# Seven-product jobs for the first half of layer 0's MLP, with the S5 tables built elsewhere

## The chip, the cores and the metric

The kernel runs on one core of one Trainium2 chip. The metric is the device time of one execution in microseconds (us). Before the change the median of 3 runs is 1545.18 us (1544.69 to 1546.54).

The core's engines work side by side, each through its own instruction list in order: PE (TensorE, matrix products into PSUM banks), DVE (VectorE), ACT (ScalarE), POOL (GpSimd) and SP (SyncE, which here only issues DMAs). An instruction that waits for another engine holds up all that stands behind it on its own engine.

## The reference

One inference step of a trunk with two layers over 544 columns (a prompt of 512 positions and 8 samples of 4), model width 1024. Layer 0 mixes tokens with a convolution module, layer 1 with a diagonal complex state-space layer (S5); each layer then has a cross-attention to a memory and an MLP with squared ReLU. All in fp32.

```python
def _s5(u, h0_re, h0_im, a_re, a_im, log_dt, b_re, b_im, c_re, c_im, d_skip, w_glu):
    dt = jnp.exp(log_dt.astype(f32))[:, None]
    mag = jnp.exp(dt * a_re)
    ab_re = mag * jnp.cos(dt * a_im)
    ab_im = mag * jnp.sin(dt * a_im)
    den = a_re * a_re + a_im * a_im
    num_re = ab_re - 1.0
    coef_re = (num_re * a_re + ab_im * a_im) / den
    coef_im = (ab_im * a_re - num_re * a_im) / den
...
def _sqrelu_mlp(xn, w_up, w_down):
    h = jax.nn.relu(jnp.einsum('bld,df->blf', xn, w_up))
    return jnp.einsum('blf,fd->bld', h * h, w_down)

def _trunk(x, conv_bufs, s5_re, s5_im, mem_k, mem_v, p):
    for i in range(DEPTH):
        h = _rmsnorm(x, p['norm_mix'][i])
...
        x = x + out
        x = x + _cross_attention(_rmsnorm(x, p['norm_xattn'][i]), mem_k[i], mem_v[i],
                                 p['xattn_w_q'][i], p['xattn_w_o'][i])
        x = x + _sqrelu_mlp(_rmsnorm(x, p['norm_ffn'][i]), p['mlp_w_up'][i], p['mlp_w_down'][i])
```

The powers of `ab` that S5's block form needs (its tables) depend on weights alone, and the kernel works them out while another stage runs.

## The kernel before

Activations lie transposed: the model width as 8 tiles of 128 partitions (`kt`, or `o` on the output side), the 544 columns along the free side. An fp32 product is made of three passes over pairs of a high and a low part (fp32r). A weight block of 128x1024 therefore gives 48 matmuls of 128x272 (8 k-tiles, 3 passes, 2 halves of the columns): this is called a gemm here.

**Weight blocks.** `run` (L140) goes through a written-out list of `Step`s. SP loads blocks of 512 KB into 6 buffers `wst` (L163), 4 blocks ahead of preparing. `prep_block` (L166) prepares a block up to two steps ahead: ACT copies the high part (L137), DVE subtracts for the low part (L177), into one of three `whl` tiles. After each step `pop_bg` lets background generators emit work up to a budget, `bg`, in their own units (about us of DVE).

**Attention.** q steps, then score steps, then the output product: `ofirst` (o = 0, 1) and `ofin(o)` (o = 2 to 7). Each `ofin` ends with `oend`: DVE adds the product to `x` (L1020), `norm_in` gives the MLP's input (ACT high part, DVE L253) and adds squares into `acc` (L262). The norm's statistic is a copy of `acc`'s last 32 columns on DVE (L284, `accs`) and a product with ones on PE (L287).

**MLP.** In layer 0 `mlp_layer` runs two halves, each 16 `up` gemms and 16 `dn` gemms. In layer 1 `seven_layer` does it with a seven-product scheme: a pair of up blocks takes 7 products of 12 matmuls (L1295) in place of 96 matmuls; the first pair stays plain (L1382); down gemms are at L1403. The sums of weights (L1176), low parts (L1168) and forms of the input (L1140 to L1143, L250) are DVE work. `us_early` prepares the first of them while the attention ends. All this is a list of jobs with an engine and a duration, put in order by a list scheduler (`planned`) whose order depends on the jobs' durations, not on the rest of the program.

**S5's tables.** `s5_prep` is a generator that runs as background in layer 0's MLP, at 3.2 a step from the first up step on. First come 143 small DVE operations on 128x32 (the scalars: dt, exponentials, sines, powers, `coef`, `unit`; L1590 to L1667). Then for each of 8 k-tiles: products on DVE (L1738 to L1763), 8 transposes on PE (L1780), 16 small matmuls (L1788), ACT copies, and rotations on DVE (L1813 to L1817, 7 levels of 4 operations, each level twice as wide). Three DMAs store E, Tst and C (L1801 to L1803), a fourth the rotations (L1819), to the DRAM tensor `tab`, which the S5 stage loads again.

## Time and profile before

| | |
|---|---|
| median of 3 runs | 1545.18 us |
| profiled execution | 1544.75 us |
| its span (first to last instruction) | 1543.0 us |
| PE busy | 1496.6 us, 97% |
| DVE busy | 1015.6 us, 66% |
| ACT busy | 685.0 us, 44% |
| POOL busy | 200.9 us, 13% |

The profiled execution is 1.75 us longer than its span. A busy share is a mean over the whole span; what an edit is worth is read in its own stretch. The stretches, in us from the start: layer 0's attention from 283 to 374.67 (from the scores on), then its output product and first MLP half to 615.17, the second half to 818.73, where the S5 stage begins; layer 1's output product and first two of four MLP quarters from 1113.82 to 1342.53. In timelines x48 is a number of instructions drawn together, and [1.82 <-ACT whl L137] the idle time ahead of them with what ended it.

### The profile page before, as it was taken

The page shows a single profiled execution, that of the slowest core. Times are in us where ns is not written, and L with a number is a line of the kernel's source. Part 1 is how long each engine was busy: PE and PEld are TensorE (multiplying, and loading weights), DVE is VectorE, ACT ScalarE, POOL GpSimd, SP SyncE. Part 2 cuts the span into 40 slices and gives each one's busy share as a digit, 9 for nine tenths or more (in the row PEclk, how much of TensorE's full clock was granted, in tenths as well). Part 3 has the DMA queues.
Part 4 walks back from the last instruction along what each step waited for, and adds up shares of the span by engine and source line. Part 5 has one row for each costly group of instructions (what it writes and reads, how often), then busy time and mean ns, then how long its engine had stood idle before and what let it go on. Part 6 is the DMA issues. An engine that isn't in the chain of part 4 may idle for free.

```text
span 1543.0 us, 29397 instructions
## 1 busy us (share of the span) xinstructions
PE 1496.6 (97%) x11949; PEld 1450.0 (94%) x11949; DVE 1015.6 (66%) x2094; ACT 685.0 (44%) x1274; POOL 200.9 (13%) x167
## 2 busy tenths in 40 slices
PE   8999979999999999999999999999999999999996
PEld 8999969898999999999998899998899999999996
DVE  6896786444576666666757964553479677685855
ACT  6332354343445433665443443343357445272642
POOL 2555550000000000000103750000000000000001
PEclk9999989999999999999999999999999999999998
DMA  8765526453223344433587974237322314141211
GB/s 278 191 156 136 185 82 219 150 220 133 101 83 103 134 134 134 134 134 116 170 271 226 340 237 182 110 138 271 125 69 85 135 55 151 42 146 47 92 46 59
DMA packets 92535, 224.49 MB, mean 145 GB/s; under 512 B 12496, under 2 KB 42976, under 8 KB 88304
## 3 DMA queue, kind: packets, MB, share of 16 engines
q1 hardware_dynamic: 87440, 211.06, 40.1%
q0 software_dynamic: 1792, 6.37, 2.3%
q10 hardware_dynamic: 3168, 5.18, 0.9%
q8 instruction: 94, 1.54, 0.4%
q14 instruction: 41, 0.34, 0.1%
HBM read 192.78 MB, written 29.80 MB: 144 GB/s over the span
## 4 chain that ended last, share of the span: by engine, by line
PE 78%; DVE 8%; ACT 1%; issue 1%; DMA 1%; POOL 0%; SPq 0%; DVEq 0%; POOLq 0%; ACTq 0%
PE banks L215 44%; PE banks L1403 12%; PE banks L1295 10%; PE banks L467 2%; PE banks L956 2%; PE banks L892 2%; PE banks L973 1%; PE banks L876 1%; PE banks L227 1%; PE banks L1382 1%; DVE banks L1958 1%; ACT slot L137 1%; DVE banks L702 1%; PE banks L1992 1%; PE banks L1780 0%
## 5 line engine op out<-in xcount | busy, mean ns | idle before, releaser
L215 PE MATMUL banks<-slot,whl 128*128 128x272 f32 x6264 | 805.0, 290 | 6.1 <-ACT slot L137 2.9
L215 PEld LDWEIGHTS banks<-slot,whl 128*128 128x128 f32 x6264 | 794.0, 189 | 11.4 <-ACT slot L137 4.8
L137 ACT ACTIVATE whl<-wst 128x1024 fp32r<-128x1024 f32 (+1 forms) x236 | 218.7, 930 | 132.8 <-PE banks L1403 47.8
L177 DVE TENSOR_TENSOR whl<-wst,whl 128x1024 fp32r<-128x1024 f32 x137 | 169.6, 1242 | 92.8 <-ACT whl L137 91.0
L1403 PE MATMUL banks<-slot,whl 128*128 128x272 f32 x912 | 120.2, 288 | 0.5 <-DVE rt L1316 0.5
L137 ACT ACTIVATE slot<-banks 128x512 fp32r<-128x512 f32 (+7 forms) x132 | 60.3, 480 | 135.5 <-PE banks L215 42.3
L1403 PEld LDWEIGHTS banks<-slot,whl 128*128 128x128 f32 x912 | 116.7, 188 | 0.7 <-DVE rt L1316 0.7
L1295 PE MATMUL banks<-slot,whl 128*128 128x272 f32 x756 | 97.2, 288 | 0.9 <-DVE tmp L1413 0.9
L1295 PEld LDWEIGHTS banks<-slot,whl 128*128 128x128 f32 x756 | 95.6, 188 | 1.1 <-ACT whl L137 1.1
L137 ACT ACTIVATE slot<-x,vec 128x544 fp32r<-128x544 f32 (+2 forms) x50 | 35.2, 727 | 108.7 <-DVE x L2027 43.8
L1413 DVE TENSOR_TENSOR tmp<-banks,rb 128x544 f32<-128x544 f32 x30 | 21.7, 724 | 83.0 <-PE banks L1403 83.0
L1403 PE MATMUL banks<-slot,arena_mlp 128*128 128x272 f32 x528 | 71.5, 288 | 0.4 <-DVE rt L1316 0.4
L1485 POOL MEMSET slot<- 128x128 f32 x1 | 0.2, 205 | 546.9 <-PE banks L1295 546.9
L702 DVE SCALAR_TENSOR_TENSOR banks<-slot,vec,banks 128x512 f32<-128x512 f32 x90 | 67.9, 755 | 2.8
L1403 PEld LDWEIGHTS banks<-slot,arena_mlp 128*128 128x128 f32 x528 | 68.2, 188 | 0.6 <-DVE rt L1316 0.6
L1295 PE MATMUL banks<-slot,arena_mlp 128*128 128x272 f32 x504 | 65.3, 288 | 0.4 <-DVE acc L1330 0.4
L1295 PEld LDWEIGHTS banks<-slot,arena_mlp 128*128 128x128 f32 x504 | 63.9, 188 | 0.7 <-DVE acc L1330 0.6
L137 ACT ACTIVATE tmp<-x 128x544 f32<-128x544 f32 x40 | 25.9, 648 | 65.0 <-DVE x L1099 39.7
L425 POOL TENSOR_TENSOR slot<-slot,slot 128x512 fp32r<-128x512 f32 x4 | 6.1, 1557 | 371.4 <-ACT slot L137 371.4
L137 ACT ACTIVATE tmp<-banks 128x544 f32<-128x544 f32 x32 | 19.9, 623 | 76.5 <-PE banks L215 76.5
L177 POOL TENSOR_TENSOR whl<-wst,whl 128x1024 fp32r<-128x1024 f32 x19 | 45.2, 2383 | 55.2 <-ACT whl L137 55.2
L250 DVE TENSOR_TENSOR slot<-tmp,slot 128x544 fp32r<-128x544 f32 x32 | 23.2, 726 | 41.5 <-ACT slot L137 41.5
(283 smaller groups left out, 2068.8 us busy)
## 6 DMA issues: line engine op xcount, KB each, us to landing
wst<-in_w SPq DMA_DIRECT2D x231, 512.0 KB, 4.4
arena_att<-in_kc SPq DMA_DIRECT2D x16, 1024.0 KB, 4.9
arena_att<-in_vc SPq DMA_DIRECT2D x16, 1024.0 KB, 5.3
tab<-arena_prep SPq DMA_DIRECT2D x24, 512.0 KB, 3.9
whl<-in_w POOLq DMA_DIRECT2D x12, 512.0 KB, 6.2
arena_s<-tab SPq DMA_DIRECT2D x8, 768.0 KB, 5.5
arena_s<-tab SPq DMA_DIRECT2D x8, 512.0 KB, 6.3
arena_s<-tab SPq DMA_DIRECT2D x12, 256.0 KB, 5.2
```

The lines of the kernel that those rows point to most:

```text
L137: self.nc.scalar.activation(out, in_, func, **kw)
L177: eng.tensor_sub(t[:, 1].bitcast(F32R), src, t[:, 0])
L215: self.nc.tensor.matmul(ps[:, c, :HALF], w, x[:, c * HALF : c * HALF + HALF], start=first and n == 0, stop=last and n == len(seq) - 1)
L227: self.nc.tensor.matmul(ps[:, c, :HALF], self.w8(b, kt)[wi], rhs[kt][xi].bitcast(F32R)[:, c * HALF : c * HALF + HALF], start=first and kt ...
L250: self.nc.vector.tensor_sub(l.bitcast(F32R), src_h if src_l is None else src_l, h)
L467: nc.tensor.matmul(ps[m], self.memt(2 * kp + k2, xi)[:, m * 128 : m * 128 + 128], t[:, wi, k2 * 512 : k2 * 512 + 512], start=kp == 0 and k ...
L702: nc.vector.scalar_tensor_tensor(A, win(k), w(k), A, op0=ALU.mult, op1=ALU.add)
L892: nc.tensor.matmul(o, qs[qi], ks[ki], start=e == 0 and i == 0, stop=e == 1 and i == 2)
L956: nc.tensor.matmul(ps[e], vs[vi], xs[xi], start=m == 0 and i == 0, stop=m == 1 and i == 2)
L1295: nc.tensor.matmul(bank, u[:, wi, k * 128 : k * 128 + 128], x[k][xi].bitcast(F32R), start=n == k == 0, stop=n == 2 and k == 3)
L1403: nc.tensor.matmul(ps[:, c, :HALF], us[kt // 4][:, wi, kt % 4 * 128 : kt % 4 * 128 + 128], M["h"][kt][xi].bitcast(F32R)[:, c * HALF : c * ...
L1413: job("V", 0.7, lambda: V.tensor_mul(self.c2(t), self.psv(ps), self.c2(self.rb)), [*bk, "rb"], [("t", o % 2)])
```

## The change

- Layer 0's first MLP half (up blocks 0 to 15, down blocks of the first half) becomes `seven_layer(0, 2)`, two quarters of the scheme of layer 1; the second half stays `mlp_layer`. The forms of the input and `us_early` now also run in layer 0's `ofin`. The up weights of that half are laid out on the host as layer 1's are.
- The scalars become a generator of their own, `s5_scalars`, background in layer 0's attention at 2.0 a step (q steps and `ofin` steps); a `pop_all` step empties it before the MLP. It uses two slots in place of the arena.
- The tables, `s5_prep`, run in the second half alone, at 5.8 a step.
- The rotations go to POOL: per k-tile 2 memsets and 28 operations, issued at the k-tile's start, and their DMA is issued there too, ahead of the k-tile's other three.

```diff
@@ oend, ofirst, ofin (layer 0 too) @@
-            if L and o % 2:
+            if o % 2:
                 self.seven_forms(o // 2)
...
-                if L and o > 5:
+                if o > 5:
                     self.us_early(2 * (o - 5))
@@ mlp_layer @@
-        for half in range(2):
-            self.steps += [up(16 * half + i) for i in range(16)]
-            self.steps += [dn(half, o, c) for o in range(8) for c in range(2)]
+        self.steps += [up(16 + i) for i in range(16)]
+        self.steps += [dn(1, o, c) for o in range(8) for c in range(2)]
@@ seven_layer @@
-    def seven_layer(self):
+    def seven_layer(self, L, quarters):
...
-        for q in range(4):
+        for q in range(quarters):
@@ s5_prep, at the start of each k-tile @@
+            W = nc.gpsimd
+            W.memset(rot[:, 0, :, 0:1], 1.0)
+            W.memset(rot[:, 1, :, 0:1], 0.0)
+            for lev in range(7):
+                n = 1 << lev
+                u = un[:, :, lev, qs].unsqueeze(3).to_broadcast([P, 2, 4, n])
+                m = rt[:, : 8 * n].rearrange("p (x q c) -> p x q c", x=2, q=4)
+                turn = lambda x: rot[:, x, :, 0:n].unsqueeze(1).to_broadcast([P, 2, 4, n])
+                new = rot[:, :, :, n : 2 * n]
+                W.tensor_mul(m, turn(1), u)
+                W.tensor_mul(new, turn(0), u)
+                W.tensor_sub(new[:, 0], new[:, 0], m[:, 1])
+                W.tensor_add(new[:, 1], new[:, 1], m[:, 0])
+            nc.sync.dma_start(tab[:, 2560:3584].rearrange("p (x q c) -> p x q c", x=2, q=4), rot)
@@ s5_prep, at the end of each k-tile @@
-            V.memset(rot[:, 0, :, 0:1], 1.0)
-            V.memset(rot[:, 1, :, 0:1], 0.0)
-            yield 0.2
-            for lev in range(7):
-                n = 1 << lev
...
-                V.tensor_mul(m[0], rot[:, :, :, 0:n], ub[0])
-                V.tensor_mul(m[1], rot[:, :, :, 0:n], ub[1])
-                yield 0.2 + 0.016 * n
-                V.tensor_sub(rot[:, 0, :, n : 2 * n], m[0][:, 0], m[1][:, 1])
-                V.tensor_add(rot[:, 1, :, n : 2 * n], m[0][:, 1], m[1][:, 0])
-                yield 0.2 + 0.008 * n
-            nc.sync.dma_start(tab[:, 2560:3584].rearrange("p (x q c) -> p x q c", x=2, q=4), rot)
@@ the program @@
-        begin, _, steps = self.att_layer(0, 0)
+        begin, _, steps = self.att_layer(0, 2.0)
         S.append(begin)
+
+        def background(work):
+            return Step(lambda: self.bgq.append(work()))
+        S.append(background(self.s5_scalars))
         S += steps
-
-        def start_prep():
-            self.bgq.append(self.s5_prep())
-        S.append(Step(start_prep))
-        self.mlp_layer(0, lambda k: self.sumsq(k, self.X[k]), 3.2)
+        S.append(Step(self.pop_all))
+        self.seven_layer(0, 2)
+        S.append(background(self.s5_prep))
+        self.mlp_layer(0, lambda k: self.sumsq(k, self.X[k]), 5.8)
```

The first place is DVE at the end of layer 0's attention. `x_74` is the last of the 8 `x` tiles, `accs` the copy for the norm's statistic. Before:

```order
L1020 TENSOR_TENSOR x_74<-x_74,banks 128x544
L253 SCALAR_TENSOR_TENSOR slot_4112<-x_74,vec,slot_4111 128x544
L262 TENSOR_TENSOR acc<-acc,tmp_87 128x544
L177 TENSOR_TENSOR whl_82<-wst_79,whl_82 128x1024
L284 COPY accs<-acc 128x4x4 x2
```

And now, from the two last rows of the work on the weights that stands behind `x_74`'s; `unit` and the two slots are the scalars':

```order
L1168 TENSOR_TENSOR arena_mlp_3821<-wst_78,arena_mlp_3821 128x512
L1168 TENSOR_TENSOR arena_mlp_3821<-wst_77,arena_mlp_3821 128x512
L1628 TENSOR_TENSOR slot_2716<-slot_2715 128x32
L1628 TENSOR_TENSOR slot_2715<-unit 128x32 x2
L1628 TENSOR_TENSOR unit<-slot_2715 128x32
L1689 COPY unit<-slot_2716 128x32
...
L1628 TENSOR_TENSOR slot_2716<-slot_2715 128x32
L1628 TENSOR_TENSOR slot_2715<-unit 128x32 x2
L1628 TENSOR_TENSOR unit<-slot_2715 128x32
L1689 COPY unit<-slot_2716 128x32
L284 COPY accs<-acc 128x4x4 x2
```

19 scalar operations now stand between the last row of `us_early` and L284, and 53 more behind the evacuations of o = 2 to 6 (10, 10, 11, 11, 11).

The second place is DVE at the last q step of layer 0's attention, where the attention norm's statistic is taken; `qz` holds copies of the query. Before:

```order
L177 TENSOR_TENSOR whl_82<-wst_76,whl_82 128x1024
L850 TENSOR_TENSOR slot_2766<-banks,slot_2765 128x544
L858 COPY qz_92<-banks 128x4x2 x4
L284 COPY accs<-acc 128x4x4 x2
L316 TENSOR_SCALAR sm_ms<-banks 128x5
```

Now:

```order
L856 TENSOR_TENSOR slot_2781<-banks,slot_2780 128x544
L864 COPY qz_92<-banks 128x4x2 x4
L1612 TENSOR_SCALAR slot_2715<-slot_2715 128x32 x2
L1614 TENSOR_SCALAR slot_2715<-slot_2715 128x32
L1648 CAST slot_2715<-slot_2715 128x32
L1612 TENSOR_SCALAR slot_2715<-slot_2715 128x32
L1628 TENSOR_TENSOR slot_2715<-slot_2715 128x32
L1628 TENSOR_TENSOR slot_2715<-slot_2715,slot_2716 128x32 x2
L1614 TENSOR_SCALAR slot_2715<-slot_2715 128x32
L1612 TENSOR_SCALAR slot_2715<-slot_2715 128x32
L1624 SCALAR_TENSOR_TENSOR slot_2715<-slot_2715 128x32
L284 COPY accs<-acc 128x4x4 x2
```

Here 11 scalar operations stand between the copies of the query and L284.

The third place is SP in the tables of one k-tile. Before, the rotations' DMA is L1819:

```order
L163 DMA wst_76<-in_w 128x1024
L163 DMA wst_77<-in_w 128x1024
L163 DMA wst_78<-in_w 128x1024
L163 DMA wst_79<-in_w 128x1024
L1801 DMA tab<-arena_prep 128x1024
L1802 DMA tab<-arena_prep 128x512
L1803 DMA tab<-arena_prep 128x8x128
L163 DMA wst_80<-in_w 128x1024
L163 DMA wst_75<-in_w 128x1024
L1819 DMA tab<-arena_prep 128x1024
```

Now it is L1779 and waits for POOL:

```order
L1757 DMA qz_91<-in_s5bc 128x256
L1779 DMA tab<-arena_prep 128x1024
L163 DMA wst_79<-in_w 128x1024
L163 DMA wst_80<-in_w 128x1024
L163 DMA wst_75<-in_w 128x1024
L1846 DMA tab<-arena_prep 128x1024
L1847 DMA tab<-arena_prep 128x512
L1848 DMA tab<-arena_prep 128x8x128
```

Three weight loads now stand behind each k-tile's rotations in SP's list.

## Rows read from the trace of the kernel before

**Rows 1.** The page: busy time, share and instructions of each engine; and the lines of the chain of work that ended last.

```profile
PE 1496.6 (97%) x11949; PEld 1450.0 (94%) x11949; DVE 1015.6 (66%) x2094; ACT 685.0 (44%) x1274; POOL 200.9 (13%) x167
PE 78%; DVE 8%; ACT 1%; issue 1%; DMA 1%; POOL 0%; SPq 0%; DVEq 0%; POOLq 0%; ACTq 0%
```

**Rows 2.** Windows: the stretch, its length, busy time (and instructions) of each engine, PE's granted clock, DMA share, GB/s. First layer 0's output product with its first MLP half, then its second half, then layer 1's output product with two quarters.

```profile
374.67:615.17 240.50, 240.50 (x1960) 239.11 (x1959) 156.54 (x456) 104.00 (x197) 0.00 (x0) 1.00 0.33 112
615.17:818.73 203.56, 201.67 (x1634) 200.07 (x1634) 127.29 (x320) 105.48 (x223) 6.32 (x6) 0.99 0.50 165
1113.82:1342.53 228.71, 224.14 (x1780) 223.03 (x1779) 165.76 (x298) 114.16 (x204) 0.00 (x0) 1.00 0.25 86
```

**Rows 3.** Timeline of DVE at the end of layer 1's attention: start, duration, what it is, idle time before it.

```profile
1131.12 0.71 DVE L1020 TENSOR_TENSOR x<-x,banks 128x544 f32<-128x544 f32 x1
...
1143.10 0.72 DVE L1020 TENSOR_TENSOR x<-x,banks 128x544 f32<-128x544 f32 x1 [0.28 <-PE banks L215]
1144.64 0.79 DVE L253 SCALAR_TENSOR_TENSOR slot<-x,vec,slot 128x544 fp32r<-128x544 f32 x1 [0.82 <-ACT slot L137]
...
1155.16 0.72 DVE L1020 TENSOR_TENSOR x<-x,banks 128x544 f32<-128x544 f32 x1 [1.86 <-PE banks L215]
...
1162.37 0.25 DVE L284 COPY accs<-acc 128x16 f32<-128x16 f32 x2
```

**Rows 4.** Timeline of PE at the same place.

```profile
1124.69 30.43 PE L215 MATMUL banks<-slot,whl 128*128 128x272 f32 x240 [1.82 <-ACT whl L137]
...
1162.93 0.36 PE L287 MATMUL banks<-ones,accs 128*128 128x2 f32 x2
```

**Rows 5.** Timeline of DVE in the scalars; nine other rows of lines L1606 and L1667 lie between the two, and the stretch from the start of the first to the start of the second has 14 operations.

```profile
466.50 0.18 DVE L1667 COPY unit<-arena_prep 128x32 f32<-128x32 f32 x1
...
468.91 0.17 DVE L1667 COPY unit<-arena_prep 128x32 f32<-128x32 f32 x1
```

**Rows 6.** Timeline of DVE and PE at layer 0's attention statistic.

```profile
284.46 0.24 DVE L284 COPY accs<-acc 128x16 f32<-128x16 f32 x2
...
283.77 1.05 PE L287 MATMUL banks<-ones,acc 128*128 128x2 f32 x8
284.76 0.38 PE L287 MATMUL banks<-ones,accs 128*128 128x2 f32 x2
```

**Rows 7.** Timeline of PE at the tables' transposes and small matmuls, of one k-tile in the first half and of one in the second; the last row is the second half's first gemms.

```profile
761.00 1.22 PE L1780 MATMUL banks<-ident,arena_prep 128*128 128x128 f32 x8 [1.89 <-ACT arena_prep L137]
...
607.51 1.03 PE L1780 MATMUL banks<-ident,arena_prep 128*128 128x128 f32 x8
608.30 6.28 PE L215 MATMUL banks<-slot,whl 128*128 128x272 f32 x48
614.51 0.67 PE L1788 MATMUL banks<-arena_prep 128*32 128x128 f32 x16
615.10 21.13 PE L215 MATMUL banks<-slot,whl 128*128 128x272 f32 x166
```

**Rows 8.** Windows of 2 us behind the idle time at 759 and behind that at 1122.87; the columns are those of rows 2.

```profile
761.00:763.00 2.00, 2.00 (x13) 2.00 (x14) 1.98 (x6) 1.98 (x6) 0.00 (x0) 0.71 1.03 296
763.00:765.00 2.00, 2.00 (x11) 2.00 (x11) 1.81 (x2) 1.38 (x2) 0.00 (x0) 0.50 0.93 340
765.00:767.00 2.00, 2.00 (x17) 2.00 (x17) 0.64 (x1) 0.00 (x0) 0.00 (x0) 0.94 0.07 27
...
1126.00:1128.00 2.00, 2.00 (x18) 2.00 (x17) 1.66 (x2) 0.30 (x1) 0.00 (x0) 1.00 0.52 184
```

**Rows 9.** Timeline of DVE in the tables: the low part of the first up product of the second half; the start of a k-tile's first table operation and of the work behind its 14th; the start of its 15th and of the work behind its 22nd.

```profile
623.48 0.73 DVE L250 TENSOR_TENSOR slot<-tmp,slot 128x544 fp32r<-128x544 f32 x1 [1.37 <-ACT slot L137]
...
595.82 0.22 DVE L1738 TENSOR_TENSOR arena_prep<-qz,arena_prep 128x64 f32<-128x64 f32 x1
...
598.99 1.23 DVE L177 TENSOR_TENSOR whl<-wst,whl 128x1024 fp32r<-128x1024 f32 x1
...
760.13 0.42 DVE L1752 TENSOR_TENSOR arena_prep<-qz,spw 128x256 f32<-128x256 f32 x1
...
763.02 1.23 DVE L177 TENSOR_TENSOR whl<-wst,whl 128x1024 fp32r<-128x1024 f32 x1
```

**Rows 10.** Groups of POOL's instructions: line, what it is, count, busy time and mean of one in ns; and one line's smallest, median and largest.

```profile
L632 POOL TENSOR_TENSOR slot<-slot,vec 128x496 f32<-128x496 f32 x10 | 11.7, 1187 | 2.9 <-DVE slot L538 2.9
...
L1971 POOL TENSOR_TENSOR sm<-slot,slot x16: 196/205/1190, 843.7 to 906.8; 128x4 f32<-128x4 f32 x16
```

**Rows 11.** Timeline of POOL and DVE at a place where both work: from the second row to the third DVE does four rotation operations of the widest level (two of 128x512, two of 128x256); then DVE alone with the same four.

```profile
745.46 6.11 POOL L425 TENSOR_TENSOR slot<-slot,slot 128x512 fp32r<-128x512 f32 x4 [371.39 <-ACT slot L137]
...
745.61 1.70 DVE L1813 TENSOR_TENSOR arena_prep<-arena_prep,unit 128x512 f32<-128x512 f32 x1
...
751.79 1.22 DVE L177 TENSOR_TENSOR whl<-wst,whl 128x1024 fp32r<-128x1024 f32 x1
...
787.34 0.69 DVE L1813 TENSOR_TENSOR arena_prep<-arena_prep,unit 128x512 f32<-128x512 f32 x1
...
789.35 1.22 DVE L177 TENSOR_TENSOR whl<-wst,whl 128x1024 fp32r<-128x1024 f32 x1
```

**Rows 12.** The page's DMA issues: count, KB each, median us from issue to landing.

```profile
wst<-in_w SPq DMA_DIRECT2D x231, 512.0 KB, 4.4
...
tab<-arena_prep SPq DMA_DIRECT2D x24, 512.0 KB, 3.9
```

More of the change, by code (lines that the diff above doesn't have):

```diff
@@ L102, in __init__ @@
         self.weave = deque()
+        self.seven = {}
         self.late = []
@@ L140, in run @@
     def run(self):
-        flat = self.flat = [b for s in self.steps for b in s.blocks]
-        npz, used = self.npz, 0
+        flat, used = self.flat, 0
         for s in self.steps:
-            used += len(s.blocks)
-            while npz < len(flat) and npz < used + self.NHL - 1 + s.deep and self.whl:
-                self.load_upto(npz + 1)
-                self.prep_block(flat[npz], npz)
-                npz += 1
-            self.load_upto(npz + self.ahead)
+            used += len(s.blocks) + len(s.raw)
+            while self.npz < self.limit and self.npz < used + self.NHL - 1 + s.deep and self.whl:
+                self.load_upto(self.npz + 1)
+                self.prep_block(flat[self.npz], self.npz)
+                self.npz += 1
+            self.load_upto(self.npz + self.ahead)
             s.fn()
@@ L160, in load_upto @@
     def load_upto(self, n, eng=None):
-        while self.nd < min(n, len(self.flat)):
+        while self.nd < min(n, self.limit):
             i = self.nd
@@ L359, in start @@
         nc, I = self.nc, self.I
-        self.flat = [b for s in self.steps for b in s.blocks]
+        self.flat, self.bases = [], []
+        for s in self.steps:
+            if s.raw:
+                self.bases.append(len(self.flat))
+            self.flat += s.blocks + s.raw
+        self.limit = self.bases[0]
         self.nd = 0
@@ L1250, in loads @@
         def loads():
-            while st["nub"] < len(self.ublocks) and ulast[st["nub"] - self.NST] < st["nu"]:
+            while st["nub"] < len(ublocks) + (0 if L else self.NST) and ulast[st["nub"] - self.NST] < st["nu"]:
                 g = st["nub"]
@@ L1257, in makes @@
             loads()
-            while st["nu"] < min(upto, len(self.uitems)):
+            while st["nu"] < min(upto, len(uitems)):
                 n = st["nu"]
-                kind, g, _ = self.uitems[n]
+                kind, g, _ = uitems[n]
                 w0, w1 = wkey(g), wkey(g + 1)
@@ L1414, in dn @@
             job("V", 0.7, lambda: V.tensor_add(self.X[o], self.X[o], t), [("t", o % 2)], [("x", o)])
-            if q == 3:
+            if L and q == 3:
                 t1 = ("t", 1 - o % 2)
@@ L1422, in seven_layer @@
         self.acc_e, self.acc_f = self.acc[:, lo], self.acc[:, hi]
-        for q in range(4):
+        for q in range(quarters):
             ps = list(range(4 * q, 4 * q + 4))
@@ L1721, in s5_prep @@
         rot = take(1, 1024).rearrange("p (x q c) -> p x q c", x=2, q=4)
+        rt = take(0, 512)
         nc.gpsimd.memset(gc, 0.0)
```

98 lines of the change are left out of this document (59 added, 39 removed).

## The prediction

> **What bounds the kernel now.** I read the page's busy times first, then the chain of waits, then windows of the stretches that change, then the timelines of PE and DVE at their edges. PE is busy for 97% of the span and makes up 78% of the chain [rows 1], so PE work saved is time saved, and an edit on another engine counts only where PE stands still for it. In the first MLP half of layer 0 PE doesn't stand still at all: 240.50 us busy of 240.50; in the second half it idles 1.89 us; in layer 1's equal stretch, which already runs the seven-product jobs, 4.57 of 228.71 [rows 2]. DVE looks free by share, 66%, but its work is bunched: at the end of layer 1's attention it waits for PE only twice between 1131 and 1162.37, for 0.28 and 1.86 us; its other pauses, 0.82 each, lie inside an evacuation, between L1020 and L253, where nothing that stands behind it can go [rows 3]. PE's product with `accs` starts 0.31 us after DVE's copy has ended (1162.62 and 1162.93), so DVE is just in time there [rows 3, 4]. The changed program puts 72 scalar operations into that very place of layer 0.
>
> **Attention.** 71 of the 143 scalars go into the q steps; where they fill DVE's pauses they cost nothing. Not so the 11 ahead of L284: the copy starts at 284.46 and PE's product with it at 284.76, while PE's products before it end at about 284.8 [rows 6], so the cover is about 0.1 us. A scalar takes 2.41 us / 14 = 0.172 us, start to start [rows 5]. That is 11 x 0.172 = 1.9, less 0.1: **+1.8**. After a stop of PE of this size the granted clock may fall: behind the 1.89 us at 759 three windows of 2 us show 0.71, 0.50 and 0.94, a loss of 2 x (0.29 + 0.50 + 0.06) = 1.7 us; behind the 1.82 us that end at 1124.69 the window shows 1.00 [rows 4, 7, 8]. 0.50 is the 1.2 GHz level, 1.00 the 2.4 GHz one. Two stops of one size with two answers: I take half, **+0.85**, bounds 0 and 1.7.
>
> **First half.** Layer 1's stretch is the model, its idle time included: 228.71 against 240.50 is -11.8 [rows 2]. In this the PE pieces of four k-tiles' tables are gone too; they come back below. Of the 72 scalars behind the evacuations of `ofin`, 72 x 0.172 = 12.4 us, DVE's two waits for PE take 0.28 + 1.86 = 2.1 [rows 3, 5]; the other 10.2 us make L284 late and PE with it, since PE has only the plain pair ahead and then needs `accs`. That gives **-11.8 + 10.2 = -1.6**. The bounds of the delay are 0 (all hidden, if layer 0's attention leaves DVE further ahead than layer 1's) and 12.4. A stop of this length costs the clock at least what the shorter one did: **+1.7** [rows 8].
>
> **Second half.** The four k-tiles moved here bring their PE pieces: 0.79 for the transposes (607.51 to 608.30) and 0.59 for the small matmuls (614.51 to 615.10) [rows 7], four times 1.38 = +5.5. What goes is the 1.89 us stop at 759 and its 1.7 of clock: there DVE's rotations were slowed by POOL and the transposes came late [rows 7, 11]; the rotations leave DVE. Together **+1.9**.
>
> For the first k-tile, all 22 table operations stand behind the first up product, and the transposes behind the second. The low part of a product ends 3.0 us after its gemm (623.48 + 0.73 against 615.10 + 6.09; a gemm is 30.43 / 5 = 6.09) [rows 4, 7, 9]. The transposes need the first 14 operations, 3.17 us (595.82 to 598.99) [rows 9]: ready 6.2 us after the first gemm, when the second ends at 6.09. Alone that is no stop. But POOL rotates for the first k-tile at the same time, and beside POOL a DVE operation took 1.70 us instead of 0.69 [rows 11]; if four or five of the 14 meet one of POOL's wide operations, the stop is 4.8. I take the middle, **+2.4**, and again half a fall of the clock, **+0.85**.
>
> For the other seven k-tiles the question is whether POOL and DVE fit beside each other. POOL: 28 operations over 24 x 127 = 3048 elements; 0.205 us for 4 elements and 1.187 for 496 make about 0.2 us plus 0.002 an element [rows 10], so 5.6 + 6.1 = 11.7 us a k-tile. DVE in the same three steps: 22 table operations 3.17 + 2.89 (760.13 to 763.02), three low parts of weights at 1.22 and three of products at 0.73 [rows 9]: 11.9 us. The three steps last 3 x 6.09 + 1.38 = 19.7. Where both worked, four operations of each took 6.33 us (745.46 to 751.79), although DVE alone needs 2.01 for its four (787.34 to 789.35) and POOL 4 x 1.22 = 4.9 [rows 10, 11]: 0.92 of the sum, nearly in turn. In turn throughout, a k-tile would take 0.92 x 23.6 = 21.7, 2.0 more than it has, 7 x 2.0 = 14. The other end is 0: they meet only in part, and the transposes have a gemm to spare from the second k-tile on. The row on turns holds only for operations that meet; half of POOL's are under 0.3 us. I take 0.5 us a k-tile, about **+4**.
>
> In the Trainium skill, SBUF — State Buffer, section "Who interferes with whom", an operation of VectorE with two inputs in SBUF and one of GpSimd that reads SBUF block each other for a whole instruction. The trace agrees but for a tenth: 0.92 of the sum and not all of it [rows 11]. By the rule in full a k-tile would take 23.6 us, and the seven 7 x 3.9 = 27 in place of 4.
>
> SP's list gets a wait: the rotations' DMA waits for POOL, with three weight loads behind it. A load has about four steps, 24.4 us, less 4.4 to landing, less a step in part until its buffer is free: some 16 us to spare as an estimate [rows 4, 12]. POOL's round is 11.7 + 3.9 for its store [rows 12] = 15.6, under 19.7, so the wait costs nothing as long as POOL isn't slowed by more than 4 us a k-tile.
>
> **The sum.** 1.8 + 0.85 - 1.6 + 1.7 + 1.9 + 2.4 + 0.85 + 4 = +11.9. The profiled execution's 1544.75 (0.43 under the median of the runs) becomes 1556.7; I say **1557 us**.
>
> **The rivals.**
> A, faster: the scalars fit. DVE is idle for a third of the span, the operations are short, and if they all end up in pauses, only -11.8 and +1.9 are left: -9.9, or 1535. For it speaks the share; against it that each scalar stands in DVE's list ahead of what PE waits for, with the pauses elsewhere [rows 3, 6].
> B, within the measurement (0.2%, 3.1 us, is about what it can tell from no change): the delays of the scalars as above, but no fall of the clock and no stop at the tables: 1.8 - 1.6 + 1.9 = +2.1, or 1547. For it speaks the full clock at 1126 [rows 8] and the gemm to spare; against it the half clock at 763.
> C, much slower, one mechanism: POOL and DVE take turns in the second half, and from the point where POOL's slowed round with its store passes 19.7 us, SP holds the weight loads. The turns alone give 14 for 4, 1567. With the store behind them a round is 21.7 + 3.9 = 25.6, 5.9 too long; seven of them are 41, less the 16 to spare 25: 1578. For it speaks rows 11, against it that half of POOL's operations are short and DVE has pauses in which POOL runs alone.
>
> **How the numbers follow.** The forecast (1550 to 1562) 0.46, A 0.12, B 0.17, C 0.25. A is faster by over 0.2%; B is mostly within it, with some of its weight to either side; C and the forecast are slower: faster 0.12, same 0.14, slower 0.74. The range leaves out A's better part and the worse end of C: 1540 to 1571.
>
> **What would show it.** In the attention, L284 behind 11 scalars and PE idle about 1.8 us ahead of the product with `accs`. At the MLP's start, PE idle some 10 us in all, at the last `ofin` gemms, the plain pair and `accs`, with DVE at work without a pause, then a window of 0.50. From the first output product after the attention to the first gemm of the second half about 240.6 us in place of 240.50. In the second half, PE idle ahead of the first k-tile's transposes, DVE table operations lengthened while POOL works, POOL about 12 us a k-tile, SP not waited for. I am wrong if PE does not wait at `accs`, if POOL's operations with broadcast inputs cost other than the rows say, or if whole gemms wait for weights behind the rotations' DMA.

## The result, and the profile after

The changed kernel takes 1564.02 us (median of 4 runs, 1561.54 to 1564.86), the kernel before 1544.93 on the same chip: ratio 1.0114, with a 95% interval of [1.0099, 1.0129]: **19 us slower**. The profiled execution took 1561.54 with a span of 1559.7, 16.8 more than the 1544.75 of before. Below is its page: each engine's busy time, and the chain of work that ended last.

```profile
PE 1495.5 (96%) x11865; PEld 1447.0 (93%) x11865; DVE 1063.3 (68%) x2024; ACT 712.3 (46%) x1364; POOL 311.3 (20%) x407
PE 71%; DVE 10%; ACT 3%; issue 2%; POOL 2%; DMA 1%; SPq 0%; DVEq 0%; POOLq 0%; ACTq 0%
```

Beside [rows 1]: 84 matmuls are gone, PE's busy time fell by only 1.1 us, and PE's part of the chain fell from 78% to 71%. Work left PE and waits took its place. DVE has 70 instructions fewer and is busy 48 us longer.

Windows of the two stages, with the columns of [rows 2]. The edges are the first gemm of layer 0's output product, the first of the second half, and the first product of the memory behind it.

```profile
378.32:619.19 240.87, 228.86 (x1780) 227.41 (x1778) 168.42 (x358) 110.03 (x197) 3.01 (x6) 0.97 0.24 82
619.19:834.15 214.96, 208.65 (x1728) 205.20 (x1729) 150.24 (x261) 127.01 (x314) 116.87 (x243) 0.99 0.57 190
```

With before's edges at 374.50, 615.10 and 818.57, the time by stage is:

| stage | before | after | difference | forecast |
|---|---|---|---|---|
| up to layer 0's output product | 374.50 | 378.32 | +3.82 | +2.65 |
| output product and first half | 240.60 | 240.87 | +0.27 | +0.1 |
| second half | 203.47 | 214.96 | +11.49 | +9.15 |
| the rest of the span | 724.43 | 725.55 | +1.1 | 0 |

The sum is 16.7 against the 11.9 forecast. PE's timeline shows where it stood still (start, duration, instruction, idle time ahead and what ended it):

```profile
286.99 0.38 PE L287 MATMUL banks<-ones,accs 128*128 128x2 f32 x2 [1.88 <-DVE accs L284]
389.41 31.98 PE L215 MATMUL banks<-slot,whl 128*128 128x272 f32 x240 [1.87 <-ACT whl L138]
422.93 6.58 PE L1383 MATMUL banks<-slot,arena_mlp 128*128 128x272 f32 x48 [1.53 <-ACT arena_mlp L138]
436.81 0.59 PE L287 MATMUL banks<-ones,accs 128*128 128x2 f32 x2 [6.52 <-DVE accs L284]
...
634.62 1.06 PE L1826 MATMUL banks<-ident,arena_prep 128*128 128x128 f32 x8 [3.07 <-DVE arena_prep L1807]
774.52 1.10 PE L1826 MATMUL banks<-ident,arena_prep 128*128 128x128 f32 x8 [1.34 <-ACT arena_prep L138]
796.39 37.93 PE L215 MATMUL banks<-slot,whl 128*128 128x272 f32 x288 [1.90 <-ACT whl L138]
```

The first and the fourth are the scalars: PE waits for a statistic that DVE copies only after them. The second is a wait of the scheme's own; layer 1 has it too (1.82, [rows 4]). The fifth is the first k-tile's transposes. The last two stand at the end of the last k-tile.

### The profile page after: what moved, and what is told of

Same layout as the page of the kernel before. It is cut to its first block, busy times and chain, and to the rows that moved or that the text cites. A ratio compares the mean times of both kernels' runs of the same rounds, so it can differ in the third digit from the quotient of the medians.

```text
span 1559.7 us, 29545 instructions
## 1 busy us (share of the span) xinstructions
PE 1495.5 (96%) x11865; PEld 1447.0 (93%) x11865; DVE 1063.3 (68%) x2024; ACT 712.3 (46%) x1364; POOL 311.3 (20%) x407
## 4 chain that ended last, share of the span: by engine, by line
PE 71%; DVE 10%; ACT 3%; issue 2%; POOL 2%; DMA 1%; SPq 0%; DVEq 0%; POOLq 0%; ACTq 0%
PE banks L215 27%; PE banks L1404 18%; PE banks L1296 14%; PE banks L898 2%; PE banks L962 2%; PE banks L473 2%; PE banks L1383 1%; ACT slot L138 1%; PE banks L979 1%; PE banks L882 1%; PE banks L227 1%; DVE banks L1988 1%; DVE whl L177 1%; ACT arena_prep L138 1%; DVE banks L708 1%
## 5 line engine op out<-in xcount | busy, mean ns | idle before, releaser
L215 PE MATMUL banks<-slot,whl 128*128 128x272 f32 x4728 | 614.0, 291 | 10.5 <-ACT whl L138 6.7
L215 PEld LDWEIGHTS banks<-slot,whl 128*128 128x128 f32 x4728 | 602.6, 190 | 16.3 <-ACT whl L138 7.6
L138 ACT ACTIVATE whl<-wst 128x1024 fp32r<-128x1024 f32 (+1 forms) x237 | 205.0, 871 | 150.5 <-PE banks L1404 96.1
L1404 PE MATMUL banks<-slot,whl 128*128 128x272 f32 x1368 | 180.7, 288 | 1.0 <-DVE rt L1317 1.0
L1404 PEld LDWEIGHTS banks<-slot,whl 128*128 128x128 f32 x1368 | 175.1, 188 | 1.5 <-DVE rt L1317 1.5
L177 DVE TENSOR_TENSOR whl<-wst,whl 128x1024 fp32r<-128x1024 f32 x103 | 131.4, 1283 | 55.5 <-ACT whl L138 54.3
L1296 PE MATMUL banks<-slot,whl 128*128 128x272 f32 x1116 | 143.8, 289 | 0.9 <-DVE tmp L1414 0.9
L1296 PEld LDWEIGHTS banks<-slot,whl 128*128 128x128 f32 x1116 | 141.4, 189 | 1.1 <-ACT whl L138 1.1
L1414 DVE TENSOR_TENSOR tmp<-banks,rb 128x544 f32<-128x544 f32 x46 | 33.3, 725 | 134.8 <-PE banks L1404 134.8
L1404 PE MATMUL banks<-slot,arena_mlp 128*128 128x272 f32 x840 | 113.6, 288 | 0.4 <-DVE rt L1317 0.4
L1404 PEld LDWEIGHTS banks<-slot,arena_mlp 128*128 128x128 f32 x840 | 108.5, 188 | 0.6 <-DVE rt L1317 0.6
L1296 PE MATMUL banks<-slot,arena_mlp 128*128 128x272 f32 x732 | 95.1, 289 | 0.8 <-DVE acc L1331 0.8
L1296 PEld LDWEIGHTS banks<-slot,arena_mlp 128*128 128x128 f32 x732 | 92.9, 188 | 1.4 <-DVE acc L1331 1.3
L138 ACT ACTIVATE rt<-rt 128x272 f32<-128x272 f32 (+1 forms) x136 | 67.1, 502 | 15.2 <-DVE rt L1317 7.7
L1168 DVE TENSOR_TENSOR whl<-wst,whl 128x512 fp32r<-128x512 f32 x101 | 68.6, 686 | 3.2 <-ACT whl L138 2.8
L138 ACT ACTIVATE arena_mlp<-wst 128x512 fp32r<-128x512 f32 x69 | 42.4, 625 | 48.9 <-PE banks L1404 40.1
```

Of the source, the lines that this page charges most:

```text
L138: self.nc.scalar.activation(out, in_, func, **kw)
L177: eng.tensor_sub(t[:, 1].bitcast(F32R), src, t[:, 0])
L215: self.nc.tensor.matmul(ps[:, c, :HALF], w, x[:, c * HALF : c * HALF + HALF], start=first and n == 0, stop=last and n == len(seq) - 1)
L1168: self.nc.vector.tensor_sub(u[:, 1].bitcast(F32R), self.us_src(n), u[:, 0])
L1296: nc.tensor.matmul(bank, u[:, wi, k * 128 : k * 128 + 128], x[k][xi].bitcast(F32R), start=n == k == 0, stop=n == 2 and k == 3)
L1404: nc.tensor.matmul(ps[:, c, :HALF], us[kt // 4][:, wi, kt % 4 * 128 : kt % 4 * 128 + 128], M["h"][kt][xi].bitcast(F32R)[:, c * HALF : c * ...
```

## The experiments

The theory on record: the scalars make DVE late at the two statistics, and POOL's rotations make DVE late in the second half. The rivals were the clock alone, SP's waits, and the seven-product jobs themselves. "More" and "less" are against the changed kernel's 1564.02; a ratio, with its interval, is against the kernel before on the same chip. Where two kernels' medians lie within some 3 us (experiments 2, 4, 6 and 9), the intervals overlap and the difference is not clear of noise; there the traces are read. Kernel 5 is that of experiment 5, and so on.

**1. The scalars out of the MLP's start.** All budget goes to the q steps from the third on.

```diff
-            return Step(fn, [("q", L, o)], bg)
+            return Step(fn, [("q", L, o)], 4.8 if bg and o > 1 else 0)
-            return Step(fn, [("o", L, o)], bg)
+            return Step(fn, [("o", L, o)], 0.0 if bg else 0)
```

> All 143 scalar operations stand in the six q steps behind the attention's statistic (24 a step), none ahead of it and none behind the output product. Theory (the scalars stood ahead of what PE waits for): the stop ahead of the product with accs in the attention (1.88 us, and 1.7 us of clock behind it) goes, and in the first MLP half the stop at accs (6.52) with most of the idle time ahead of it and its half clock goes: from the first output product to the second half's first gemm about 230 us in place of 240.9. Together about -14: 1550 us against after's 1564. If the q steps can't hold 24 operations (4.1 us), new stops of 1 to 2 us a step appear there. Rival (the jobs start badly in layer 0 for another reason, such as the weights): only the attention's 3.6 us go, 1560.

Measured: 1557.92, 1.0080 [1.0065, 1.0095], 6.1 less instead of 14. The place was right, the count wrong: the program has 162 scalar operations, not the 143 that I had counted. So 18 stayed ahead of `accs`, and the attention steps got stops of their own. PE's timeline of this kernel:

```profile
329.37 1.07 PE L979 MATMUL banks<-arena_att,pz 128*32 128x256 f32 x16 [1.09 <-DVE pz L931]
...
431.43 0.58 PE L287 MATMUL banks<-ones,accs 128*128 128x2 f32 x2 [3.71 <-DVE accs L284]
...
629.25 1.94 PE L1826 MATMUL banks<-ident,arena_prep 128*128 128x128 f32 x8 [3.09 <-DVE arena_prep L1807]
```

The wait at `accs` went from 6.52 to 3.71, and the stretch with the first half from 240.87 to 235.96. The last row is the stop of 3.07 again, but its eight transposes took 1.94 us where they took 1.06: here the clock fell. From them to the next k-tile's transposes it took 22.41 us (629.25 to 651.66) instead of 19.81 (634.62 to 654.43), and the second half took 217.93 instead of 214.96. The same stop comes with either answer, 2.6 us apart. This may be a part of why the median lies 2.5 above the profiled execution; it isn't shown.

**2. Only the 22 scalars ahead of the attention's statistic moved.**

```diff
-            return Step(fn, [("q", L, o)], bg)
+            return Step(fn, [("q", L, o)], 2.4 if bg and o > 1 else 0)
-            return Step(fn, [("o", L, o)], bg)
+            return Step(fn, [("o", L, o)], 2.0 if bg else 0)
```

> The scalars begin behind the attention's statistic, 12 a step in six q steps, the last 72 or so behind the output product as in after. Theory: only the stop at the statistic (1.88) and its half clock (1.7) go, everything else stays: 1560.4 us against after's 1564. Rival (PE's stop there is made good later, since PE isn't the bound in the attention): within 1 us of after.

Measured: 1561.50, 1.0099 [1.0084, 1.0114], 2.5 less. The stop of 1.88 is gone, and the output product begins 2.4 earlier (375.92). Counted from the statistic's first product (284.06 in the changed kernel, 285.14 here; executions of the same code differ by 2.1 there), it begins 3.5 earlier: the stop and its clock. The ten more scalars that fell behind the output product lengthened the wait at `accs`:

```profile
436.10 0.59 PE L287 MATMUL banks<-ones,accs 128*128 128x2 f32 x2 [8.39 <-DVE accs L284]
```

**3. No rotations at all.** POOL's loop over the levels goes.

```diff
-            for lev in range(7):
+            W.memset(rot, 0.0)
+            for lev in range(0):
```

> The 28 rotation operations on POOL of each k-tile are left out (the rotations' part of the tables is zeros); the DMA stays. Theory (POOL's rotations slow DVE's table operations and hold SP): the stops at the first k-tile's transposes (3.07), at the last k-tile's (1.34) and behind the last k-tile (1.90 and 1.7 of clock) go but for some 0.5 us, about -7: 1557 us against after's 1564. Rival (the table work itself is too much for the 24 steps, POOL beside it costs nothing): the stops stay, 1563 to 1564.

Measured: 1554.83, 1.0059 [1.0044, 1.0074], 9.2 less. Window of its second half:

```profile
621.52:829.10 207.58, 206.62 (x1729) 203.64 (x1729) 120.85 (x261) 127.36 (x314) 12.69 (x14) 1.00 0.58 197
```

DVE runs the same 261 instructions, and they take 120.85 us instead of 150.24: POOL's 104 us of rotations cost DVE 29. All stops but one of 0.96 are gone, and the stage is 7.4 shorter.

**4. The rotations' DMA behind the k-tile's other stores.** The transfer is issued on SP after the last table's.

```diff
-            nc.sync.dma_start(tab[:, 2560:3584].rearrange("p (x q c) -> p x q c", x=2, q=4), rot)
...
+            nc.sync.dma_start(tab[:, 2560:3584].rearrange("p (x q c) -> p x q c", x=2, q=4), rot)
```

> POOL rotates as in after, but the rotations' DMA is issued last in its k-tile, behind E, Tst and C and the weight loads. Theory (the stop of 1.90 us behind the last k-tile comes from SP, which waits for POOL with a DMA behind it that ACT needs): that stop and its 1.7 of clock go, -3.6: 1560.4 us. Rival (it comes from ACT's small copies of the last k-tile ahead of the weight copies, whatever SP does): 1564. The stops at the first k-tile (3.07) and at the last one's transposes (1.34) stay under both.

Measured: 1565.17, 1.0125 [1.0108, 1.0142], 1.1 more. The stop of 1.90 went, as the theory had it: ACT's copy of `x` starts 0.08 us behind DVE's L1098 (792.00 and 792.08) and waits for no store. This run alone wouldn't prove SP's wait to be the cause, since PE came later here and left ACT more time; the rows of the changed kernel below show the chain. The last transposes came later, by DVE now and with the clock down, so nothing was won:

```profile
780.18 1.94 PE L1825 MATMUL banks<-ident,arena_prep 128*128 128x128 f32 x8 [4.24 <-DVE arena_prep L1806]
```

**5. The scalars spread in three places.** Some 16 a step in the later q steps, 12 behind each partial output product, and the powers of the unit (30 operations by a shorter formula, 42 before) two at a time behind the first half's down products.

```diff
-            return Step(fn, [("q", L, o)], bg)
+            return Step(fn, [("q", L, o)], 3.2 if bg and o > 1 else 0)
-            return Step(fn, [("o", L, o)], 0, hold=True)
+            return Step(fn, [("o", L, o)], 2.4 if bg else 0, hold=True)
-            return Step(fn, [("o", L, o)], bg)
+            return Step(fn, [("o", L, o)], 0)
...
+                V.tensor_add(self.X[o], self.X[o], t)
+                if not L:
+                    self.pop_bg(0.4)
```

> No scalar operation ahead of the attention's statistic and none behind the output product: 16 a step in the six later q steps, 12 behind each of the two partial output products, and the last powers of unit (30 operations in place of 42, by a shorter formula) between the down products of the first MLP half, 2 behind each. Theory: the stop at the statistic with its clock (3.6) and, in the first half, the stop at accs (6.52), part of the one ahead of the plain pair (1.53) and the clock behind them (1.7) go, nothing new comes: -13, 1551 us against after's 1564. Rival (in scal_q6 18 operations were left ahead of accs and the first half gained only 4.9; the rest is the layer's own weights and forms): about scal_q6's 1558.

Measured: 1547.74 (10 runs), 1.0020 [1.0011, 1.0030], **16.3 less**. The output product begins at 374.69 as before the change, and the stretch behind it takes 230.66 instead of 240.87. PE's timeline:

```profile
425.36 0.38 PE L287 MATMUL banks<-ones,accs 128*128 128x2 f32 x2 [0.74 <-DVE accs L284]
...
620.78 1.07 PE L1838 MATMUL banks<-ident,arena_prep 128*128 128x128 f32 x8 [3.08 <-DVE arena_prep L1819]
```

The second half is as in the changed kernel (215.15). So the scalars' places, with the 12 operations that the formula saves, cost 3.6 in the attention and 10.2 behind it.

**6. More room for the tables.** The first k-tile's transposes one gemm later, the rotations' DMA on POOL's own queue.

```diff
+            if kt == 0:
+                yield 5.8
...
-            nc.sync.dma_start(tab[:, 2560:3584].rearrange("p (x q c) -> p x q c", x=2, q=4), rot)
+            nc.gpsimd.dma_start(tab[:, 2560:3584].rearrange("p (x q c) -> p x q c", x=2, q=4), rot)
```

> The first k-tile's transposes come one gemm later, and the rotations' DMA is issued on POOL's own queue, so SP doesn't wait for POOL; rotations still on POOL. Theory: the stop at the first transposes (3.07) goes, and the one behind the last k-tile (1.90) with its clock (1.7), since it came from SP; the one at the last transposes (about 1.3) stays: -6.7, 1557.3 us against after's 1564. Rival (DVE's and ACT's table work for the last k-tile is late in any case, as dmalast's new stop of 4.24 hints): the stop moves to the last transposes, 1560 to 1562.

Measured: 1561.87, 1.0112 [1.0095, 1.0129], 2.1 less: the rival was right. Both stops went, and PE waited at later k-tiles instead, for DVE or for ACT: 0.79, 0.28, 0.45, 0.45, 1.04, and at the last

```profile
782.11 1.90 PE L1828 MATMUL banks<-ident,arena_prep 128*128 128x128 f32 x8 [2.86 <-DVE arena_prep L1807]
```

The tables aren't late at the start alone; beside POOL they are late at each k-tile from the fourth on.

**7. The two together** (5 and 6).

> scal_split and tables together. Theory: the two gains add up, -13 - 6.7: 1544 us, level with the kernel before. Rival (not independent, or what is left is the scheme's own): 1548 or more.

Measured: 1549.69, 1.0030 [1.0018, 1.0041]; no better than 5 alone.

**8. The rotations back on DVE**, as the kernel before had them, with a budget of 7.6 a gemm instead of 5.8.

> after with the rotations back on DVE at the end of each k-tile, budget 7.6 a step. Theory: leaving the rotations out altogether gave -9.2, so POOL's slowing of DVE costs about that; on DVE they take 8.05 us a k-tile, DVE's load becomes 11.9 + 8.05 = 20 us in the 19.7 us of three steps, so about as much is lost again: 1555 to 1564. Rival A (POOL's contention is what mattered, DVE has room): 1555. Rival B (DVE becomes the bound and falls behind by more than a step): 1570 or more.

Measured: 1584.26, 1.0250 [1.0234, 1.0266], 20.2 more. The second half takes 235.44 instead of 214.96. PE's timeline, and windows (columns of [rows 2]) of one k-tile's round and of the last one:

```profile
811.87 1.94 PE L1812 MATMUL banks<-ident,arena_prep 128*128 128x128 f32 x8 [11.49 <-DVE arena_prep L1793]
...
682.38:708.21 25.83, 25.83 (x218) 25.48 (x217) 19.96 (x62) 18.34 (x43) 0.00 (x0) 1.00 0.48 158
791.56:811.87 20.31, 2.14 (x27) 1.48 (x25) 17.09 (x57) 8.98 (x30) 0.00 (x0) 0.61 0.56 178
```

The time is rival B's, but the cause is the budget. From 630.71 to 734.01 PE doesn't stand still: with 7.6 a gemm a k-tile takes four gemms instead of three, 25.8 us, and DVE works for 20.0 of them. Eight k-tiles of that length don't fit ahead of the down product at which `pop_all` empties the list, so the last two stand together at the end, with no gemm of PE between them. In a round of three gemms DVE would have some 18.0 of 19.8 us, an estimate: 19.96 less the two low parts of one gemm, 1.23 and 0.73. No run tried that, so this run doesn't show that DVE can't hold the rotations, nor that POOL saves 20 us; POOL's price of some 7 (experiment 3) stands.

**9. Five narrow levels on POOL, the two widest on DVE** behind the tables, budget 8.9.

```diff
-            for lev in range(7):
+            for lev in range(5):
...
+            for lev in range(5, 7):
```

> after with only the five narrow levels of the rotations (20 operations, up to 128 elements) on POOL, the two wide ones (8 operations) on DVE at the end of each k-tile, the DMA behind them; budget 8.9 a step, which keeps three steps a k-tile. Theory (what hurts is a DVE operation that waits for a wide POOL operation): POOL's time a k-tile falls to about 5.5 us, DVE's own rises by 3.0 to 14.9 of 19.7; the stops at the first transposes (3.07) and behind the last k-tile (1.90 and clock) shrink to under 1: -6, 1558 us against after's 1564. Rival A (any POOL operation that reads costs a turn, wide or not): 1562 or more. Rival B (DVE's added 3 us make the tables late, as in rot_dve): 1566 or more.

Measured: 1560.83, 1.0098 [1.0082, 1.0114], 3.2 less. The half's stops shrink to one, but a long one, and the half itself takes 214.30 (620.45 to 834.75), only 0.7 less than in the changed kernel; theory and rival A are not told apart by the time:

```profile
777.30 1.94 PE L1825 MATMUL banks<-ident,arena_prep 128*128 128x128 f32 x8 [5.01 <-DVE arena_prep L1806]
```

**10. Experiments 5 and 9 together.**

> scal_split with rot_mix's rotations. Theory: 1547.7 - 6 = 1541.7 us, 3.4 below the kernel before (0.2%). Rival A: 1546. Rival B: 1550.

Measured: 1546.83 (12 runs), 1.0008 [0.9997, 1.0019]: level with before, as the rival said. The stop of 5.10 stays. POOL and DVE just ahead of it:

```profile
748.28 5.44 POOL L431 TENSOR_TENSOR slot<-slot,slot 128x512 fp32r<-128x512 f32 x4
...
748.36 1.49 DVE L1865 TENSOR_TENSOR arena_prep<-arena_prep,unit 128x256 f32<-128x256 f32 x1 [1.18 <-POOL arena_prep L1790]
...
753.91 0.69 DVE L1865 TENSOR_TENSOR arena_prep<-arena_prep,unit 128x512 f32<-128x512 f32 x1
```

POOL's four low parts of the next layer's keys and values (`kv_load`, line L431) meet DVE's widest rotations. An operation of 512 columns took 0.69 behind them, one of 256 took 1.49 beside them.

**11 and 12. These four moved**, from the down product 2 to 5, behind the end of the tables: in kernel 10 (this is kernel 11), and alone in the kernel before.

```diff
-                if (L, half, o, c) == (0, 1, 2, 0):
-                    self.kv_load(lambda i: self.slot()[:, :512], nc.gpsimd)
...
+                    self.kv_load(lambda i: self.slot()[:, :512], nc.gpsimd)
```

> best2 with the memory's four low parts (POOL, 128x512 each, 5.4 us) issued at the sixth down product's step, behind the last table work, in place of the third's. Theory (best2's one stop that is left in the second half, 5.10 at the last transposes with its clock, comes from these four operations beside DVE's and ahead of POOL's last rotations): the stop and the clock go, -6.5: 1540.5 us, 0.3% under the kernel before. Rival (the down products' own DVE work makes the last table late): the stop stays at 3 us or more, 1545.

> The kernel before with the same four operations moved alone. Theory (its one stop in the second half, 1.89 at 761 with 1.7 of clock, has the same cause): -3.6, 1541.5 us. Rival (it comes from the down products' DVE work): 1545.

Measured: kernel 11 1541.94 (11 runs), 0.9975 [0.9966, 0.9984]; the kernel before with the move 1542.02 (12 runs), 0.9981 [0.9971, 0.9990]. Both beat the kernel before, whose 1545.61 on that chip is a median of 22 runs. Kernel 11's PE timeline at the place, and its stages:

```profile
757.14 1.07 PE L1836 MATMUL banks<-ident,arena_prep 128*128 128x128 f32 x8 [0.79 <-DVE arena_prep L1817]
```

```profile
375.06:604.23 229.17, 224.49 (x1780) 223.46 (x1778) 161.40 (x314) 110.38 (x197) 3.00 (x6) 1.00 0.26 86
604.23:813.18 208.95, 207.79 (x1728) 203.89 (x1729) 143.77 (x325) 127.67 (x314) 69.67 (x179) 1.00 0.58 196
```

The stop of 5.10 became 0.79, so POOL's low parts were its cause. They were also that of the 1.89 us which PE lost in the kernel before [rows 7]: with the move it loses nothing.

```profile
374.33:614.93 240.60, 240.60 (x1960) 239.21 (x1959) 156.57 (x457) 104.28 (x197) 0.00 (x0) 1.00 0.34 112
614.93:814.75 199.82, 199.82 (x1636) 198.43 (x1633) 127.26 (x320) 105.75 (x223) 6.34 (x6) 1.00 0.51 167
```

What does the seven-product half bring, then? PE's timeline of the same kernel gives the price of a k-tile's pieces:

```profile
614.93 30.43 PE L215 MATMUL banks<-slot,whl 128*128 128x272 f32 x240
645.20 1.04 PE L1779 MATMUL banks<-ident,arena_prep 128*128 128x128 f32 x8
...
652.79 30.43 PE L215 MATMUL banks<-slot,whl 128*128 128x272 f32 x240
```

A round of six gemms and one k-tile takes 652.79 - 614.93 = 37.86; five gemms take 645.20 - 614.93 = 30.27, six 36.32; the pieces are 1.54. Four of them left the first half, which would be 240.60 - 6.16 = 234.44 without the new jobs; it is 229.17, **5.3 less**. The new jobs' own stops in it (1.86, 0.75, 0.42, 0.51, 1.15 = 4.7) keep most of the rest of what 84 fewer matmuls save. The second half would be 199.82 + 6.16 = 205.98 and is 208.95, **3.0 more**: 0.79 is the stop above, and the other 2.2 PE's own rows don't show as idle time. From 604.23 kernel 11's rounds of three gemms and one k-tile start as follows (PE's timeline):

```profile
604.23 12.34 PE L215 MATMUL banks<-slot,whl 128*128 128x272 f32 x96 [1.15 <-ACT whl L138]
...
624.02 12.34 PE L215 MATMUL banks<-slot,whl 128*128 128x272 f32 x96
...
644.06 12.34 PE L215 MATMUL banks<-slot,whl 128*128 128x272 f32 x96
```

The later rounds start at 664.09, 684.13, 704.20, 724.24, 744.00 and 764.77. So the first round and the seventh take 19.79 and 19.76, and the five between them 20.03 to 20.07, 1.3 more in all. A round of 19.79 is itself 0.09 longer than three gemms and the 1.54, which makes 0.7 over eight. What holds the five is DVE. The weight loads stand still ahead of the transposes, and though the row names no releaser, DVE's timeline has one: the transposes read what L1817 writes.

```profile
635.93 0.36 DVE L1817 TENSOR_TENSOR arena_prep<-arena_prep 64x192 f32<-64x192 f32 x1
...
636.40 0.86 PEld L1836 LDWEIGHTS banks<-ident,arena_prep 128*128 128x128 f32 x8 [0.25 <-issue]
```

The load starts 0.11 us behind the end of this operation, and in the other four rounds 0.11 or 0.12 behind it (ends at 656.33, 676.35, 696.42, 716.45). In the seventh round L1817 ends 1.34 us ahead of the load, and nothing stands still. So DVE, with the two wide levels in its list, is just too late for the transposes; in kernel 5, where POOL has them, the same rounds take 19.77 or 19.78.

The two stages together are 2.3 less, and yet the medians, 1541.94 and 1542.02, show no gain. Two things stand against it. The 5.3 hold for an execution in which the clock stayed up behind the stop of 1.86; in kernels 5 and 10 the same stretch took 230.66 and 230.64, 1.5 more. And what is alike in both kernels differs between executions by as much: ahead of the attention's statistic kernel 11 is already 0.7 later (its first product starts at 284.31 against 283.61), and from the end of the second half on it takes 726.0 against 723.65, where the kept executions of all kernels take 723.65 to 726.25.

## Why the prediction was right, and where not

It said slower, 1557 in 1540 to 1571, by terms that stand in the profile one by one; the time is 1564. The direction was right, and so were the stops at the two statistics and at the first transposes. The sum was 5 short (16.7 for 11.9): the time lies outside the 1550 to 1562 of the forecast itself and nearer to C's 1567, so it is the width of the range that held it. Rival A falls with the stops at both statistics, B with the stop of 3.07 and the clock behind the first, C because the second half grew by 11.5, not by 9.15 + 10 = 19 or more. It was not far off: POOL's operations of a k-tile spread over some 15 us, and the next k-tile's begin when their store has landed, 4.4 to 5.2 later (from the third on), which about fills a round of 19.8. Its wait on SP came once, by another cause (below).

**Attention, +2.65 forecast, +3.82.** PE idled 1.88 where 1.8 was forecast, and the same edit undone gave it back with its clock (experiment 2). Of the 3.82, 0.29 arose ahead of the statistic, whose first product starts at 283.77 before and at 284.06 after, less than executions of the same code differ by. The term that was too small is "I take half" of the clock. The window of 4 us behind the stop, and that behind the same stop (1.87) in kernel 6, whose attention is the same:

```profile
288.00:292.00 4.00, 4.00 (x26) 3.70 (x19) 1.69 (x11) 0.00 (x0) 0.00 (x0) 0.57 0.70 240
...
289.00:293.00 4.00, 4.00 (x42) 3.42 (x42) 2.21 (x14) 0.00 (x0) 0.00 (x0) 1.00 0.67 240
```

0.57 over 4 us is a loss of 4 x 0.43 = 1.7, the upper bound; kernel 6 lost nothing, the lower one. Which of the two an execution gets was chance here, and half a fair guess.

**First half, +0.1 forecast, +0.27.** The sum is right by luck, since the errors of its terms cancel. With the scalars elsewhere (experiment 5) the stretch is 9.9 below before where layer 1's stretch gave 11.8; 1.5 of the difference is the clock behind the stop of 1.86 (last section). With them it is 10.2 longer, where 10.2 of delay and 1.7 of clock made 11.9. PE's idle time grew by 12.01 - 4.68 = 7.33, not 10.2 (busy 228.86 of 240.87 above; the five stops of kernel 5 are those of kernel 11 to 0.01), so 2.9 of the 10.2 is the clock. Windows at the wait for `accs`, where DVE is busy nearly throughout, PE not at all at first, and the granted clock at 0.50:

```profile
432.00:436.00 4.00, 0.00 (x0) 0.00 (x0) 3.69 (x19) 2.08 (x5) 0.00 (x0) 0.50 0.39 100
436.00:440.00 4.00, 3.19 (x14) 3.19 (x15) 3.96 (x12) 2.46 (x5) 0.00 (x0) 0.50 0.40 162
```

The delay was set too high (10.2 for 7.3) and the clock too low (1.7 for 2.9). And it was 74 scalars here, not 72.

**Second half, +9.15 forecast, +11.49.** The PE pieces are 1.54 a k-tile by the rounds above, not 1.38: the gemms next to them lengthen too, which the rows of the transposes alone didn't show. The first k-tile's stop is 3.07 for a forecast 2.4. The mechanism there is the forecast one; DVE and POOL at this place (timeline of each):

```profile
629.10 0.21 DVE L1786 TENSOR_TENSOR arena_prep<-arena_prep,coef 128x64 f32<-128x64 f32 x1
629.24 1.06 DVE L1787 TENSOR_TENSOR arena_prep<-arena_prep,coef 128x64 f32<-128x64 f32 x1
...
629.17 1.04 POOL L1775 TENSOR_TENSOR arena_prep<-arena_prep,unit 128x512 f32<-128x512 f32 x1
```

A DVE operation of 0.21 takes as long as the wide POOL operation beside it. In the Trainium skill, SBUF — State Buffer, section "Who interferes with whom", such a pair excludes each other for a whole instruction; here the trace agrees. The seven other k-tiles together had been put at +4 for turns. Six of them cost PE nothing, though POOL slowed DVE in each. At the last PE lost 1.34, of which 0.96 stays without any rotation (experiment 3), and 1.90, which came through SP. That these and the clock behind them make about the 4 of that term is luck. In all, four pieces are 6.16; a round of three gemms and a k-tile takes 19.79 where 3 x 6.05 + 1.54 would be 19.70, 0.7 more over eight; the old stop and its clock take off 1.89 + 1.7; the three new stops are 6.31; and the six gemms behind the last one took 37.76 (796.39 to 834.15) instead of 36.3, 1.5 of clock. That is 11.1 of the 11.49.

**"SP not waited for" was wrong**, for PE in one k-tile of eight. POOL was busy 13.8 us a k-tile ((311.3 - 200.9) / 8) instead of 11.7, because DVE also slows POOL, and SP waited for it four times, 25.3 us in all; but seven k-tiles' rotations were stored in time. The last ones were late for a reason that no term had: ahead of them in POOL's list stand the four low parts of `kv_load` (L431), which experiments 11 and 12 move. From the second on, POOL had begun a k-tile every 19 to 21 us, the seventh at 734.59. Then it stood idle for ACT's copies of `kv_load`, worked on the low parts, and began the eighth at 767.52, 13 us late. At the last k-tile the work on all engines reads:

```profile
762.02 5.56 POOL L431 TENSOR_TENSOR slot<-slot,slot 128x512 fp32r<-128x512 f32 x4 [12.48 <-ACT slot L138]
767.52 0.10 POOL L1767 MEMSET arena_prep<- 128x4 f32 x1
...
781.42 1.71 POOL L1778 TENSOR_TENSOR arena_prep<-arena_prep 128x256 f32<-128x256 f32 x1
...
783.16 0.32 SPq L1779 DMA_DIRECT2D tab<-arena_prep  x1
...
784.06 0.72 SPq L1104 DMA_DIRECT2D ud<-tmp  x1
784.89 0.73 DVE L1098 TENSOR_TENSOR x<-x,tmp 128x544 f32<-128x544 f32 x1
789.06 0.66 ACT L138 ACTIVATE tmp<-x 128x544 f32<-128x544 f32 x1 [11.66 <-DMA ud<-tmp]
...
790.81 4.44 ACT L138 ACTIVATE arena_prep<-arena_prep 32x32 f32<-32x32 f32 x16
...
795.28 2.01 ACT L138 ACTIVATE whl<-wst 128x1024 fp32r<-128x1024 f32 x2
```

I had priced the weight loads behind the rotations' DMA; what stood there was the store of `ud`. ACT stood idle for 11.66 us; until 785.62 it would have waited for DVE's `x` in any case, and the last 3.4 us were for the buffer of that store. The next weights came late by it, and PE stood 1.90. In experiment 4 ACT doesn't wait for the store and the stop is gone. No run moved the low parts alone in the changed kernel, so what they cost there isn't measured.

**What no term had:** the rest of the program is 1.1 longer, which is within what that part varies by between executions (723.65 to 726.25, above), and the median lies 2.5 above the profiled execution. The clock behind the stop of 3.07 can explain up to 2.6 of the latter in a run (experiment 1); this isn't shown.

## What to carry to other kernels

Work is placed by the wait it stands ahead of, not by the share of an engine that is free: the scalars cost 14 us ahead of two statistics, and 12 operations fewer of them almost nothing a few at a time behind other products. When work moves to POOL, price every DVE operation that meets it at the length of POOL's, look at what else stands in POOL's list ahead of it, and list every transfer behind POOL's on the same queue with what waits for its buffer. And before a larger change, look for the cause of the stops that are there already: the move of four POOL operations alone, in the kernel before, gave what the mended change with that move gave.
